# Splitting weight blocks with ScalarE and an adding transfer instead of VectorE, in a hybrid decoder layer

## The chip, the cores and the metric

The kernel runs on one core of a Trainium2 chip. The metric is the device time of one execution in microseconds (us); lower is better. The core has TensorE (matrix products, PE in the rows below; PEld is its weight load), VectorE (DVE), ScalarE (ACT), GpSimd (POOL) and SyncE (SP, which issues most transfers). Each engine takes its own instructions in order and waits for the others through semaphores.

## The reference

One decoder layer over 512 tokens of width 1024, in fp32. The normalised input goes through one projection (`w_in`), whose columns feed three groups of heads: NSA attention (a compressed branch, a selected branch and a window branch), RWKV-7 time mixing, and MoBA attention. Their outputs are joined by one output projection; a ConvGLU channel mixer and a final RMSNorm follow. Cut to what matters here:

```
h    = rmsnorm(x, attn_norm)
proj = h @ w_in                            # p_nsa, p_rw, p_moba
kc   = gelu(blocks(kc) @ cmp_w1[0]) @ cmp_w2[0]     # vc likewise with [1]
x    = x + concat(o_nsa, o_rw, o_moba) @ w_out
x    = x + conv_glu(rmsnorm(x, ffn_norm), ffn_w_in, ...)
out  = rmsnorm(x, final_norm)
```

With 512 tokens the selected branch takes every block and the window covers every earlier token, so the kernel computes both as causal attention.

## The kernel before, in words

Products are computed to about fp32 accuracy from a reduced-precision format (fp32r): every operand is split into a high part (the value rounded to fp32r) and a low part (the value minus its high part), and a product is three products, high by high, high by low and low by high (`mm3`, lines 240 to 242).

The weights of the layer's first half come in 70 blocks of 128 x 512 (256 KB): 38 of the input projection (19 projections of 128 columns, two blocks each), 16 of the hidden layer of the compression (8 blocks each for values, `hv`, and keys, `hk`) and 16 of the output projection. A block is loaded by SP into a tile `wraw` (six buffers). `wunit` casts it on ScalarE to the high tile `whi` (line 211, six buffers) and subtracts on VectorE to get the low tile `wlo` (line 212, five buffers). `wnext` hands the next block to whoever needs one and keeps a list of blocks already split, two long. The blocks come in the order of `ORDER`: ks, r1, v1, k1, q0, cv, ck (two each), hv (eight), q1, kw (two each), hk (eight), and then the rest; `nv` stands in between with loads and splits of its own (lines 732 and 733, tile `vw`). The first 30 blocks thus reach to the fourth block of hk.

The work of the first half is written as streams (Python generators): `w_stream` (the weight products), `rw_run` (two RWKV pairs), `cmp_attention`, `att_stream` (scores and softmax of nine pairs of heads, one after the other) and `val_stream` (their values). Each stream yields an estimate of the time until its next step (`CW`, `CATT` = 2.5 and so on), and `merge` takes the stream that is due first. The order so found is the program's order. The framework that lays out the engines' queues may still move an instruction ahead of earlier ones of its engine when its inputs are there first: the program's order is a priority, and the queues are made anew whenever an instruction changes. The same framework puts in every wait, those for a free buffer included.

Names that the text below uses: the first 16 loads (`xr`, `fraw`) and four projections run before the streams start. `s` is a score tile, `qt` the split query (line 702), written after the evacuation `P` (line 696). `Y`, `TA`, `GA`, `AR` and `Nc` belong to RWKV: `Y` (line 573) is a step of a triangular inverse; `Nc` (line 505) comes back from a round trip through memory and is used by `DvT` (line 508). `blk` holds the compression's blocks: POOL clears a column of each (line 890), VectorE fills it (line 896) and splits it (`bhl`, line 902). `ph` is the hidden layer's accumulator (lines 917 and 918). The RWKV gate products wait for a sigmoid on ScalarE (line 1062). POOL also computes reciprocal roots (lines 293, 392, 673, 862). From about 300 us on the ConvGLU mixer runs, whose splits are its own.

Of the kernel before, what the change touches and what calls it, by code (L numbers as in the profile page):

```python
# [24 lines left out]
CW, CRW0, CRW1, CATT, CVAL, CFIN, CCMP, CCA, RWLAG = 1.25, 3.45, 3.57, 2.5, 1.28, 4.05, 3.17, 1.69, 0  # L25
CT = 2.51
NR = 5
WARM = 5
KOUT, EARLY2, NEARLY2 = 1, 3, 2
LAG = 2  # L30
DMS = [0, 4, 1, 5, 2, 6, 3, 7]
# [4 lines left out]
F32 = mybir.dt.float32  # L36
F32R = mybir.dt.float32r
AF = mybir.ActivationFunctionType
OP = mybir.AluOpType
# [39 lines left out]
def cap(name):  # L79
    return CAPS.get(name, CDEF)  # L80
# [11 lines left out]
def hybrid_layer(ctx: ExitStack, tc: tile.TileContext, xT, cst, cols, lora, fgain, wA, wVn, cw1,  # L92
                 wO, wF, wG, out, dbg=None):
    nc = tc.nc
    act, dve, pool, pe, sp = nc.scalar, nc.vector, nc.gpsimd, nc.tensor, nc.sync
# [7 lines left out]
    def mark(label):  # L103
        MARKS.append((label, nc.cur_bb.bb.instructions[-1].name))
# [7 lines left out]
    def bank(name):  # L112
        live[0] += 1
        return ps.tile([128, 512], F32, name=name, bufs=pcap(name))
# [8 lines left out]
    def r2(name, shape=(128, 512), dt=F32):  # L123
        return sb.tile(list(shape), dt, name=name, bufs=cap(name))
# [69 lines left out]
    p0 = bank("rs")  # L194
    for i in range(WARM):
        pe.matmul(p0[:, 0:256], idle[:, 0:128], idle, start=True, stop=True)
# [8 lines left out]
    rcol = fixe(4)  # L205


    def wunit(raw, w):
        hi = sb.tile([128, 512], F32R, name="whi", bufs=cap("whi"))
        lo = sb.tile([128, 512], F32R, name="wlo", bufs=cap("wlo"))  # L210
        act.copy(hi[:, :w], raw)  # L211
        dve.tensor_tensor(lo[:, :w], raw, hi[:, :w].bitcast(F32), op=OP.subtract)  # L212
        return hi, lo

    def wload(src, w=512):
        raw = r2("wraw")
        sp.dma_start(raw[:, :w], src)
        return raw


    wsrc, wready = [], []
# [5 lines left out]

    def wsplit():
        src, m = wsrc.pop(0)
        wready.append(wunit(wload(src, m)[:, 0:m], m))  # L230

    def wnext():
        while len(wready) < 2 and wsrc:
            wsplit()
        return wready.pop(0)

# [23 lines left out]
    for z in SEQ:  # L260
# [13 lines left out]
        for k, i in new:  # L274
            n = sum(o[1] == i for o in order1)
# [31 lines left out]
    def proj_fm(box):  # L307
        yield from want()
        p = bank("mm")
        for u in range(2):  # L310
            hi, lo = wnext()
            for k in range(4 * u, 4 * u + 4):
                c = slice((k - 4 * u) * 128, (k - 4 * u + 1) * 128)
                mm3(p, (hi[:, c], lo[:, c]), (xh[k], xl[k]), k == 0, k == KT - 1)
                yield CW
        box.append(p)
# [457 lines left out]
    def soft(qt, kk, par, sums, mid):  # L774
        kh, kl, lo = kk
        two, three = r2("prob"), r2("prob")
        pt_ = two[:, 384:512], mid[:, par * 256:par * 256 + 256], two[:, 0:384], three
        Ps = []
        for i in range(NT):
            n = (i + 1) * 128  # L780
            yield from want()
            s_ = bank("s")
            qs = slice(i * 128, (i + 1) * 128)
            pe.matmul(s_[:, 0:n], qt[:, qs], kh[:, 0:n], start=True, stop=False)
            pe.matmul(s_[:, 0:n], qt[:, qs], kl[:, 0:n], start=False, stop=True)  # L785
            P = pt_[i]
            m = sm("m", 1)
            dve.tensor_tensor_reduce(out=P, in0=s_[:, 0:n], in1=con("cmask")[:, 512 - n:512], scale=1.0,  # L788
                                     scalar=3e38, op0=OP.add, op1=OP.min, accum_out=m)
            done()  # L790
            act.activation(P, P, AF.Exp, bias=m, scale=-1.0, accum_out=sums[:, i, par:par + 1])  # L791
            Ps.append(P)
            yield CATT
        return Ps
# [112 lines left out]
    def hidden(kv):  # L907
        while bhls[kv] is None:
            yield None
        bhl = bhls[kv]  # L910
        yield from want()
        ph = bank("ph")
        for u in range(8):
            hi, lo = wnext()
            for i in range(2):
                tp = u * 2 + i
                pe.matmul(ph[:, 0:256], bhl[tp // 4][:, tp % 4, :], hi[:, i * 256:(i + 1) * 256], start=tp == 0, stop=False)
                pe.matmul(ph[:, 0:256], bhl[tp // 4][:, tp % 4, :], lo[:, i * 256:(i + 1) * 256], start=False, stop=tp == 15)
            yield CW
        spawn(compressed(kv, ph))  # L920
# [198 lines left out]
    def w_out(part, dm, k0, k1):  # L1119
# [7 lines left out]
        for k in range(k0, k1):  # L1127
            while oT[k] is None:
                yield None
            if (k - k0) % 4 == 0:  # L1130
                hi, lo = wnext()
            c = slice((k - k0) % 4 * 128, ((k - k0) % 4 + 1) * 128)
            mm3(p, (hi[:, c], lo[:, c]), oT[k], k == k0, k == k1 - 1)
            yield CW
# [59 lines left out]
    def sums_tile():  # L1194
        return sm("sums", 8).rearrange("p (t h) -> p t h", h=2)
# [10 lines left out]
    def fin_nsa(j, b, OPt, sums, ob):  # L1206
        mark(f'fnsa{j}.{b}')
        c = sm("coef", 8)
        cv = c.rearrange("p (t h) -> p t h", h=2)
        dve.reciprocal(cv, sums)  # L1210
        o1 = 6 * j + b
        dve.tensor_tensor(cv, cv, gates[:, :, o1:o1 + 4:3], op=OP.mult)
        t = yield from scaled(OPt, c)
        ob.append(t)
        if len(ob) < 2:
            return
        while not cadone[0]:
            yield None
        yield CFIN
        at('ob').tensor_tensor(ob[0], ob[0], ob[1], op=OP.add)  # L1220
        yield from want()
        oc = bank("oc")
        for i in range(NT):
            pe.matmul(oc[:, i * 128:(i + 1) * 128], PT[j][:, i, :], Vbd[j], start=True, stop=True)
        yield CFIN
        dve.tensor_tensor(ob[0], ob[0], oc, op=OP.add)
        done()
        yield CFIN
        yield from finish_pair(ob[0], col("nsa_gain", j), j)

    def fin_moba(j, OPt, sums):
        mark(f'fmoba{j}')
        r = sm("coef", 8)
        dve.reciprocal(r, sums.rearrange("p t h -> p (t h)"))
        t = yield from scaled(OPt, r)
        yield CFIN
        yield from finish_pair(t, col("moba_gain", j), 5 + j)

    def att_stream():
        for kind, j, b in HEADS:  # L1240
            fold = ENG[f"F{kind}{j}{b}"] == 'p'
            OPt, sums = (r2("OPt"), r2("OPt") if fold else None, fold), sums_tile()
            if b < 2:
                ob = []
            while len(queue) > QMAX:
                yield None
            Ps, vs, mid = [], [], r2("prob")
            for par in range(2):
                h = 2 * j + par
                if kind == "n":  # L1250
                    kk = (ks, kw)[b - 1]
                    while qn[h] is None or not kk or not vn:
                        yield None
                    q_, k_, v_ = qn[h], kk[h // 3], vn[(b - 1) * 2 + h // 3]
                else:
                    while j not in mq or j not in mk or j not in mv:
                        yield None
                    q_, k_, v_ = mq[j][par], mk[j][par], mv[j][par]
                mark(f'soft{kind}{j}.{b}.{par}')
                vs.append(v_)  # L1260
                P = yield from soft(q_, k_, par, sums, mid)
                Ps.append(P)
            fin = fin_nsa(j, b, OPt, sums, ob) if kind == "n" else fin_moba(j, OPt, sums)
            queue.append((Ps, vs, OPt, fin, f'{kind}{j}.{b}'))
        queue.append(None)
# [14 lines left out]
    spawn(rw_run(0))  # L1280
    spawn(cmp_attention())
    spawn(att_stream())
    spawn(val_stream())
    merge()
# [267 lines left out]
```

## Time and profile before

| | us |
|---|---|
| median of 3 runs | 730.33 (729.77 to 731.89) |
| the profiled execution, its own time | 731.48 |
| its span in the profile | 729.4 |
| TensorE busy | 705.4 (97%) |
| VectorE busy | 627.0 (86%) |
| ScalarE busy | 415.3 (57%) |
| POOL busy | 30.8 (4%) |

The span is the profiled execution from its first to its last recorded instruction. A busy time counts an engine's instructions without overlap; the rest of the span is idle. The mean granted clock of TensorE was 0.986 of full speed. In the rows a name like `wlo<-wraw,whi` is output and inputs, `x30` a count, and what stands behind `<-` in brackets is what ended an idle time.

### The profile page before, as it was taken

What the parts mean: (1) busy time and instruction counts of PE and PEld (TensorE: products, weight loads), DVE (VectorE), ACT (ScalarE), POOL (GpSimd) and SP (SyncE); (2) the same over time, 40 slices, a digit from 0 to 9 for tenths busy, and PEclk for the clock granted to TensorE, in tenths of its full rate; (3) what the DMA queues carried; (4) which work ended last, traced back from release to release, by engine and by line L of the source; (5) the groups of instructions that cost most, each with busy time, mean ns of one, the idle gap of its engine ahead of it and who ended that gap; (6) DMA issues with size and microseconds to landing.
All of it is one profiled execution on the core that took longest, in us unless ns stands there. A gap on an engine that the chain in (4) does not pass through costs nothing. (4 is left out here: it accounts for less than half of the span.)

```text
span 729.4 us, 13565 instructions
## 1 busy us (share of the span) xinstructions
PE 705.4 (97%) x5156; PEld 613.6 (84%) x5156; DVE 627.0 (86%) x1377; ACT 415.3 (57%) x862; POOL 30.8 (4%) x46
## 2 busy tenths in 40 slices
PE   9999988899999999999999999999999999999995
PEld 6777867678788788888899899999999999998884
DVE  6579679878897999797999999999999999999804
ACT  8475434465656877774766546455564555657403
POOL 4010100000000000011000000000000000000001
PEclk9989989999999999999999999999999999999999
DMA  9622021513110022024246333323333333346003
GB/s 328 193 87 80 13 50 49 140 65 117 44 44 30 1 59 73 30 72 145 74 144 218 97 107 102 116 87 102 97 108 101 102 103 110 98 126 201 1 1 115
DMA packets 44800, 69.86 MB, mean 96 GB/s; under 512 B 10688, under 2 KB 12352, under 8 KB 44736
## 3 DMA queue, kind: packets, MB, share of 16 engines
q1 hardware_dynamic: 44016, 67.95, 29.4%
q10 hardware_dynamic: 720, 1.06, 0.4%
q8 instruction: 40, 0.66, 0.4%
q14 instruction: 24, 0.20, 0.1%
HBM read 64.40 MB, written 4.59 MB: 95 GB/s over the span
## 5 line engine op out<-in xcount | busy, mean ns | idle before, releaser
L1301 ACT CAST ah<-S 128x512 fp32r<-128x512 f32 x88 | 54.5, 621 | 57.6 <-DVE S L1296 57.6
L240 PE MATMUL mm<-xh,whi 128*128 128x512 f32 x152 | 69.6, 458 | 0.0
L241 PE MATMUL acc<-dn,dn 128*128 128x512 f32 (+1 forms) x173 | 64.3, 372 | 0.0
L242 PE MATMUL acc<-dn,dn 128*128 128x512 f32 (+1 forms) x173 | 63.8, 371 | 0.0
L242 PE MATMUL mm<-xh,wlo 128*128 128x512 f32 x152 | 61.8, 406 | 0.0
L241 PE MATMUL mm<-xl,whi 128*128 128x512 f32 x152 | 61.5, 404 | 0.0
L1302 DVE TENSOR_TENSOR al<-S,ah 128x512 fp32r<-128x512 f32 x88 | 58.7, 682 | 0.7 <-ACT ah L1301 0.6
L791 ACT ACTIVATE prob<-prob,fixed 128x128 f32<-128x128 f32 (+1 forms) x72 | 40.5, 563 | 28.5 <-DVE fixed L788 26.5
L240 PE MATMUL acc<-dn,dn 128*128 128x512 f32 (+1 forms) x173 | 54.9, 371 | 0.0
L211 ACT CAST whi<-wraw 128x512 fp32r<-128x512 f32 x70 | 42.6, 618 | 19.8 <-PE mm L241 14.1
L212 DVE TENSOR_TENSOR wlo<-wraw,whi 128x512 fp32r<-128x512 f32 x70 | 47.3, 682 | 3.6 <-PE mm L242 2.2
L240 PE MATMUL pB<-bh,ah 128*128 128x256 f32 x172 | 50.1, 291 | 0.1
L242 PE MATMUL pB<-bh,al 128*128 128x256 f32 x172 | 48.6, 283 | 1.1 <-DVE al L1302 1.0
L242 PE MATMUL pC<-bh,al 128*128 128x256 f32 x172 | 48.5, 282 | 0.3 <-DVE al L1302 0.3
L240 PE MATMUL pC<-bh,ah 128*128 128x256 f32 x172 | 48.5, 282 | 0.2 <-ACT ah L1301 0.2
L241 PE MATMUL pB<-bl,ah 128*128 128x256 f32 x172 | 48.3, 281 | 0.0
L241 PE MATMUL pC<-bl,ah 128*128 128x256 f32 x172 | 48.1, 280 | 0.0
L1302 DVE TENSOR_TENSOR al<-wraw,ah 128x512 fp32r<-128x512 f32 x66 | 43.4, 681 | 0.0
L823 ACT CAST ph<-pt 128x512 fp32r<-128x512 f32 (+3 forms) x72 | 29.7, 425 | 23.3 <-PE pt L816 22.4
L788 DVE CUSTOM_DVE_ANT_0 prob<-s,early 128x128 f32<-128x128 f32 (+1 forms) x72 | 34.7, 483 | 6.6 <-PE s L785 5.0
L1301 ACT CAST ah<-wraw 128x512 fp32r<-128x512 f32 x66 | 36.8, 618 | 1.4 <-DVE x L1135 1.3
L241 PEld LDWEIGHTS acc<-dn,dn 128*128 128x128 f32 x173 | 32.6, 188 | 5.3 <-DVE dn L1365 0.2
(400 smaller groups left out, 2211.8 us busy)
## 6 DMA issues: line engine op xcount, KB each, us to landing
wraw<-in_wF_dram SPq DMA_DIRECT2D x88, 256.0 KB, 2.7
wraw<-in_wG_dram SPq DMA_DIRECT2D x44, 256.0 KB, 3.0
wraw<-in_wA_dram SPq DMA_DIRECT2D x38, 256.0 KB, 3.0
xr<-in_xT_dram SPq DMA_DIRECT2D x16, 256.0 KB, 4.1
wraw<-in_cw_dram SPq DMA_DIRECT2D x16, 256.0 KB, 3.3
wraw<-in_wO_dram SPq DMA_DIRECT2D x16, 256.0 KB, 2.6
fraw<-in_wA_dram SPq DMA_DIRECT2D x8, 256.0 KB, 5.2
x2d<-x2o SPq DMA_DIRECT2D x8, 256.0 KB, 3.3
```

Of the source, the lines that this page charges most:

```text
L211: act.copy(hi[:, :w], raw)
L212: dve.tensor_tensor(lo[:, :w], raw, hi[:, :w].bitcast(F32), op=OP.subtract)
L240: pe.matmul(o, ah, bh, start=first, stop=False)
L241: pe.matmul(o, ah, bl, start=False, stop=False)
L242: pe.matmul(o, al, bh, start=False, stop=last)
L788: dve.tensor_tensor_reduce(out=P, in0=s_[:, 0:n], in1=con("cmask")[:, 512 - n:512], scale=1.0, scalar=3e38, op0=OP.add, op1=OP.min, accum_ ...
L791: act.activation(P, P, AF.Exp, bias=m, scale=-1.0, accum_out=sums[:, i, par:par + 1])
L823: act.copy(h, t_[:, 0:n])
L1301: act.copy(h, src)
L1302: at(f'L{i}').tensor_tensor(l, src, h.bitcast(F32), op=OP.subtract)
```

## The change

For the first 30 blocks VectorE's subtraction goes. ScalarE multiplies the block by -1 into `wlo` (which rounds it, so that `wlo` holds minus the high part), and POOL issues a transfer that adds the block, read from memory a second time, onto `wlo`. `wnext` keeps four blocks split instead of two; this holds for all 70 blocks. And `att_stream` yields two more steps of `CATT` before the scores of its first head.

```
+NADD, WAHEAD = 30, 4
...
-    def wunit(raw, w):
+    wcnt = [0]
+
+    def wunit(raw, w, src):
         hi = sb.tile([128, 512], F32R, name="whi", bufs=cap("whi"))
         lo = sb.tile([128, 512], F32R, name="wlo", bufs=cap("wlo"))
         act.copy(hi[:, :w], raw)
-        dve.tensor_tensor(lo[:, :w], raw, hi[:, :w].bitcast(F32), op=OP.subtract)
+        wcnt[0] += 1
+        if wcnt[0] <= NADD:
+
+            act.mul(lo[:, :w], raw, -1.0)
+            pool.dma_start(lo[:, :w], src.bitcast(F32R), accum_op=OP.add)
+        else:
+            dve.tensor_tensor(lo[:, :w], raw, hi[:, :w].bitcast(F32), op=OP.subtract)
         return hi, lo
...
-        wready.append(wunit(wload(src, m)[:, 0:m], m))
+        wready.append(wunit(wload(src, m)[:, 0:m], m, src))
 
     def wnext():
-        while len(wready) < 2 and wsrc:
+        while len(wready) < WAHEAD and wsrc:
...
                     q_, k_, v_ = mq[j][par], mk[j][par], mv[j][par]
+                if (kind, j, b, par) == ("n", 0, 1, 0):
+
+                    yield 2 * CATT
                 mark(f'soft{kind}{j}.{b}.{par}')
```

## Rows read from the trace of the kernel before

**Rows 1.** The page: busy time of TensorE and VectorE, share of the span.
```profile
span 729.4 us, 13565 instructions
PE 705.4 (97%) x5156; PEld 613.6 (84%) x5156; DVE 627.0 (86%) x1377; ACT 415.3 (57%) x862; POOL 30.8 (4%) x46
```

**Rows 2.** Stages: length, busy PE, PEld, DVE, ACT, POOL (instructions), clock, transfer share, GB/s.
```profile
20.00:170.00 150.00, 140.96 (x1278) 112.48 (x1277) 115.83 (x297) 78.09 (x161) 5.50 (x8) 0.94 0.30 84
20.00:50.00 30.00, 28.86 (x124) 21.99 (x123) 17.61 (x35) 19.38 (x34) 3.05 (x2) 0.89 0.46 138
90.00:110.00 20.00, 16.66 (x167) 12.48 (x166) 13.43 (x33) 7.37 (x15) 0.00 (x0) 0.83 0.24 51
110.00:140.00 30.00, 25.44 (x341) 20.78 (x340) 27.99 (x82) 12.96 (x30) 0.39 (x3) 0.94 0.30 82
170.00:300.00 130.00, 127.41 (x974) 104.63 (x972) 113.14 (x313) 87.95 (x228) 6.54 (x4) 1.00 0.16 49
```

**Rows 3.** TensorE's waits, 0 to 250 us: total, times, longest.
```profile
PE s L784 <- DVE qt L702: 3.9, 2, 3.3
PE ph L918 <- DVE wlo L212: 2.5, 2, 2.1
PE rw L533 <- DVE Y L573: 1.7, 1, 1.7
...
PE rw L366 <- ACT rwin L1062: 0.6, 1, 0.6
```

**Rows 4.** TensorE in order of time: start, duration, what, idle before.
```profile
131.47 0.39 PE L918 MATMUL ph<-wlo,bhl 128*128 128x256 f32 x1 [2.06 <-DVE wlo L212]
...
134.71 0.79 PE L240 MATMUL mm<-xh,whi 128*128 128x512 f32 x1
...
136.79 0.39 PE L240 MATMUL mm<-xh,whi 128*128 128x512 f32 x1
```

**Rows 5.** VectorE in order of time.
```profile
115.00 0.68 DVE L212 TENSOR_TENSOR wlo<-wraw,whi 128x512 fp32r<-128x512 f32 x1
...
118.77 0.68 DVE L573 TENSOR_TENSOR Y<-rw,Dv 128x512 f32<-128x512 f32 x1
```

**Rows 6.** All engines in order of time, around the first score product.
```profile
91.50 0.76 DVE L508 TENSOR_TENSOR DvT<-Nc,early 128x256 f32<-128x256 f32 x2 [4.78 <-DMA Nc<-s]
...
93.25 0.69 DVE L696 SCALAR_TENSOR_TENSOR P<-mm,early 128x512 f32<-128x512 f32 x1
...
95.91 0.47 PE L784 MATMUL s<-kk,qt 128*128 128x128 f32 x1 [3.34 <-DVE qt L702]
...
97.58 0.79 PE L240 MATMUL mm<-xh,whi 128*128 128x512 f32 x1
```

**Rows 7.** The two splitting lines: duration in ns (min/median/max), first and last start.
```profile
L211 ACT CAST whi<-wraw x70: 602/620/639, 17.7 to 354.0; 128x512 fp32r<-128x512 f32 x70
L212 DVE TENSOR_TENSOR wlo<-wraw,whi x70: 641/682/694, 19.8 to 365.5; 128x512 fp32r<-128x512 f32 x70
```

**Rows 8.** VectorE's instructions on `wlo` alone, one stage: busy (count), clock, transfers.
```profile
110.00:140.00 30.00, 7.44 (x11) 0.94 0.30 82
```

**Rows 9.** POOL in order of time.
```profile
30.34 1.02 POOL L293 TENSOR_TENSOR early<-fixed 128x4 f32<-128x4 f32 x1 [11.57 <-DVE fixed L292]
...
115.04 0.14 POOL L890 MEMSET blk<- 128x16 f32 x1 [32.38 <-DVE bhl L902]
```

**Rows 10.** Transfers by line: KB each, median us from issue to landing.
```profile
wraw<-in_wA_dram SPq DMA_DIRECT2D x38, 256.0 KB, 3.0
...
x2t<-x2d SPq DMA_DIRECT2D x8, 256.0 KB, 3.6
```

**Rows 11.** The hidden layers' low products: duration in ns, first and last start.
```profile
L918 PE MATMUL ph<-wlo,bhl x32: 278/281/386, 117.5 to 166.8; 128*128 128x256 f32 x32
```

**Rows 12.** TensorE in order of time: the second hidden layer's first low product.
```profile
155.02 0.28 PE L918 MATMUL ph<-wlo,bhl 128*128 128x256 f32 x1
```

**Rows 13.** ScalarE's waits for a free high tile, whole span: total, times, longest.
```profile
ACT whi L211 <- PE mm L241: 14.1, 7, 4.7
```

## The prediction

> **What bounds the kernel now.** I read the page first. TensorE is busy 705.4 us of a span of 729.4 and VectorE 627.0 [rows 1]. So TensorE's own work sets the time, and a change elsewhere can only give back what TensorE loses: time in which it stands idle, and time at half clock (the lower of its two levels, 1.2 GHz against 2.4). Next the table by stage, for the stage that the change touches, 20 to 170 us [rows 2]. TensorE is busy 140.96 of 150 there, so 9.0 us are idle. A granted clock that is 0.11 short over 30 us, 0.17 short over 20 us and 0.06 short over 30 us has cost 3.3, 3.4 and 1.8 us of work, 8.5 in sum. Those 17.5 us are all that this stage has to give. From 170 to 300 TensorE is idle 2.6 of 130 us at full clock: behind the stage there is little to win and something to lose.
>
> Third, who ends TensorE's waits in 0 to 250 us [rows 3]. Four rows carry nearly all: the first score product of attention waits for VectorE's `qt` (3.9 us, one wait of 3.3); the compression's hidden layer for `wlo`, the very subtraction that the change takes away (2.5, one of 2.1); RWKV for `Y`, VectorE too (1.7); and the LoRA gate for ScalarE's sigmoid (0.6).
>
> Last the order of time around these waits. At 131.47 us TensorE has stood 2.06 us for `wlo`, and at 134.71 a weight product takes 0.79 where the same line takes 0.39 at 136.79: the clock fell behind the gap [rows 4]. On VectorE the subtractions stand in line between RWKV's and the blocks' work, one at 115.00 ahead of the late `Y` at 118.77 [rows 5]. The gap of 3.34 us at 95.9 has another cause: VectorE stood 4.78 us for a transfer of RWKV's triangular block (`Nc`), with the query's evacuation queued behind it; the weight products that follow at 97.58 run at half speed [rows 6].
>
> **The change part by part.**
>
> *VectorE loses 30 subtractions.* One takes 0.68 us [rows 7], so 20.5 us go. Eleven of them start in the tightest stage, 110 to 140 us, where VectorE is busy 27.99 of 30 and gives up 7.44 [rows 2, 8]. What TensorE gets: the wait for `wlo`, 2.5, whole; of the 1.7 for `Y` what the subtractions ahead of it take, one or two of 0.68, say 0.9; and of the 1.8 of clock in that stage half, 0.9, since some small gaps stay. **Term 1: 4.3 us gained**; bounds 2.5 (the named wait alone) and 6.4 (all 4.6 idle and 1.8 clock).
>
> *Attention's first head begins two planner steps later.* The wait at 95.9 is that head's first product. Put behind other ready work it would cost nothing: the weight products at 97.58 waited only for their turn. At stake are the 3.3 idle and the 3.4 of clock in 90 to 110 us [rows 2, 6]. The engines' order is made anew, and neither the transfer that VectorE waited for nor its place in VectorE's order need change; between none and all I take half. **Term 2: 3.3 gained**, bounds 0 and 6.7.
>
> *ScalarE gains 30 multiplies.* The nearest row is its cast of the same tile, 0.62 us [rows 7]: 18.6 us onto the 78.1 that it is busy in 150 us [rows 2]. It stays at 64%, so its idle time hides them, except where TensorE waits for ScalarE already: the gate's sigmoid. One multiply queued ahead of it costs 0.6, three 1.9. **Term 3: 0.6 lost**, bounds 0 and 1.9.
>
> *POOL gains 30 adding transfers.* None is in the trace. POOL's part of one: the nearest row is its power of 128x4, 1.02 us [rows 9]; bounds nothing and twice that; I take 1.0. To land: a plain 256 KB load takes 3.0 us, and one that must also read its target at most two such transfers in turn, 3.0 and 3.6 [rows 10]; I take 4.0, nearer to the one transfer that it is. With the multiply a low tile takes 5.6 us to fill, against 1.3 now (cast and subtraction), bounds 3.6 and 9.3. The cover is the lookahead: four blocks ready, five `wlo` buffers. Filled in turn, five buffers give a block each 5.6 / 5 = 1.1 us (1.9 at the upper bound). TensorE asks fastest in the second hidden layer, 8 blocks from 155.0 to 166.8, 1.5 us each [rows 11, 12]; a projection's block, 12 products of 512 columns, lasts longer. At my value the cover holds. At the upper bound 12 hidden-layer blocks lose 0.4 each, 4.3 us in sum. Some one block will come late in a new order. **Term 4: 1.0 lost**, bounds 0 and 4.3. The transfers read 7.9 MB more; the DMA engines are busy 0.30 of this stage [rows 2], so that stays hidden.
>
> One rule of the Trainium skill speaks against this part ("SBUF — State Buffer", "SBUF: two separate sides"): POOL writes the descriptors of its own transfers, and is locked out of SBUF while VectorE runs a two-port operation such as an fp32 copy. No run here shows it yet. By it an add would wait out a copy, not the operations on two tensors that make up most of VectorE's time there, and the sum would stay; were the lock wider than the page says, VectorE's 93% in 110 to 140 us would make every add late there. I give the rival of late adds a little more for it.
>
> *Splits stand four blocks ahead, for all 70 blocks.* ScalarE already waits 14.1 us in seven waits for TensorE to free a `whi` buffer [rows 13]. Issued two blocks earlier against the same six and five buffers, such waits come more often, with exponentials and evacuations queued behind them. ScalarE (88 of 130 us in 170 to 300) has room; VectorE, at 113 of 130, has less. **Term 5: 1.0 lost**, bounds 0 and 3.0 (as much again as TensorE idles there now).
>
> Sum: 4.3 + 3.3 - 0.6 - 1.0 - 1.0 = 5.0 us. The profiled execution took 731.48, so 726.5; the median of the runs, 730.33, lies 1.15 below the profiled one, so **725.3**.
>
> **The rivals.**
>
> *Late adds (slower).* POOL takes its work in order, and between 82 us and the end of the first hidden layer stand three clears of `blk`, each waiting for VectorE: the first until 115.04, for 32.4 us [rows 9]. An add queued behind the first starts at 115.2 and lands at 120.2, where TensorE now reads the first hidden-layer `wlo` at 117.5 [rows 11]: 2.7 late. With the three clears, and each 2.7 to 5 late, 8 to 15 us; I take 10, and the 2.5 of term 1 is gone. That is 731.5 - 5.0 + 9.0 + 2.5 = 738.0, on the median's scale 736.9. It decides once the adds' lateness passes the gains, some 6 us. Against it: the adds' sources are ready long before, and nothing says that they stand behind the clears.
>
> *No change.* Either VectorE's relief is off the path beyond the 2.5 us named (2.5 - 0.6 - 1.0 - 1.0: 0.1 faster), or the later head pushes back attention's chain of nine heads, and the two steps of 2.5 us that term 2 borrowed are paid at its end (5.0 - 5.0). Both give 730.3. For it: VectorE's 87% in 170 to 300 us. Against: TensorE is full there, so a later head only changes what it does meanwhile.
>
> *All of it.* VectorE lighter by a fifth in the stage, all of term 1's and term 2's upper bounds come, 13.1 us: 717.2. For it: every large wait in rows 3 but the sigmoid's ends on VectorE. Against: RWKV's chain and its transfers stay.
>
> **How the numbers follow.** Forecast 0.48, all of it 0.12, no change 0.22, late adds 0.18. The forecast's own range is 722 to 728. The sum of the unfavourable bounds (2.5 + 0 - 1.9 - 4.3 - 3.0) is 6.7 slower, 737; that of the favourable ones 717.2. Cutting the outermost at both ends, the range is 717.5 to 736. A measurement of this kernel tells about 0.3%, 2.2 us, from no change: below 728.1 lie the forecast but for 0.04 and all of the third rival, 0.56; within 2.2 us lie that 0.04 and most of the no-change case, 0.20; the rest of that case and the late adds are slower, 0.24.
>
> **What would show it.** Term 1: no wait of TensorE on `wlo` in 110 to 140 us, VectorE there near 21 to 24 of 30, and a granted clock above 0.94. Term 2: the first score product without a gap of 3 us ahead of it, and a clock in 90 to 110 us near 1. Term 3: the wait for the sigmoid near 1.2. Term 4: adds that land within some 5 us and TensorE's waits on them under 1 us each. Term 5: 170 to 300 us with TensorE idle no more than 4 us. The prediction is wrong if an add takes over 9 us from multiply to landing, if POOL's clears hold the adds, or if new gaps of the reordered RWKV chain bring the clock down elsewhere.

## The result and the profile after

The changed kernel takes **734.79 us** (median of 6 runs, 732.22 to 735.62) against 730.5 for the kernel before on the same chip (6 runs, 729.77 to 731.89): a ratio of 1.0056 (95% interval 1.004 to 1.0073), some 4 us slower. The forecast was 725.3, faster; the time lies inside the forecast's range of 717.5 to 736, but on the slow side of the kernel before. The profiled execution has a span of 733.2 us, 3.8 more than before. In three kernels of the experiments (e1, e4 and e7 there) one execution took far longer than the rest (2219, 2359 and 842 us); the ratios leave these out, and the profiles of e1 and e7 are of one more execution each.

The page first, busy time and share of the span; it answers to [rows 1].

```profile
span 733.2 us, 13656 instructions
PE 706.7 (96%) x5156; PEld 613.6 (84%) x5156; DVE 610.4 (83%) x1347; ACT 431.3 (59%) x892; POOL 55.9 (8%) x76
```

VectorE has lost 16.6 us of work, ScalarE has gained 16.0 and POOL 25.1. TensorE does what it did. The stages, with the columns of [rows 2]:

```profile
20.00:170.00 150.00, 138.56 (x1272) 109.75 (x1271) 97.90 (x265) 92.32 (x190) 30.84 (x39) 0.95 0.62 139
20.00:50.00 30.00, 27.50 (x119) 21.05 (x118) 10.20 (x21) 18.20 (x33) 7.62 (x11) 0.93 0.77 187
90.00:110.00 20.00, 19.93 (x247) 15.00 (x246) 14.41 (x36) 9.51 (x20) 3.52 (x4) 1.00 0.62 106
110.00:140.00 30.00, 22.77 (x300) 18.67 (x298) 20.88 (x71) 18.43 (x39) 9.08 (x13) 0.89 0.86 183
170.00:300.00 130.00, 127.27 (x970) 104.38 (x970) 112.18 (x311) 86.66 (x224) 6.58 (x4) 1.00 0.15 48
```

In 90 to 110 us all has come that term 2 hoped for: TensorE stands 0.07 us in place of 3.34, at full clock. In 110 to 140 us VectorE is light, 20.88 in place of 27.99, and yet TensorE does less, 22.77 in place of 25.44, and the clock is 0.89 in place of 0.94. The column before the last is the news: the DMA engines are busy 0.62 of the stage in place of 0.30, 0.77 of the opening in place of 0.46, and 0.86 of 110 to 140 us in place of 0.30. What ended TensorE's waits, 0 to 400 us (total, times, longest):

```profile
PE ph L927 <- DMA wlo<-in_cw_dram: 5.7, 3, 3.5
PE rw L364 <- ACT rwin L1070: 1.7, 1, 1.7
PE rw L542 <- DVE Y L582: 1.5, 1, 1.5
...
PE rw L375 <- ACT rwin L1071: 0.8, 1, 0.8
```

The wait of the hidden layer for the subtraction [rows 3] is now one for the add, and more than twice as long. The transfers of the page: queue, packets, MB, share of 16 engines; then issues with KB each and median us to landing. The last fence holds two rows of the kernel before that are not shown above.

```profile
q1 hardware_dynamic: 44016, 67.95, 29.2%
q0 software_dynamic: 4320, 7.87, 6.5%
...
wlo<-in_wA_dram POOLq DMA_DIRECT2D x18, 256.0 KB, 7.3
wlo<-in_cw_dram POOLq DMA_DIRECT2D x12, 256.0 KB, 5.3
wraw<-in_wVn_dram SPq DMA_DIRECT2D x8, 137.0 KB, 6.4
...
early<-in_lora_dram SPq DMA_DIRECT2D x1, 128.0 KB, 11.5
```

```profile
wraw<-in_wVn_dram SPq DMA_DIRECT2D x8, 137.0 KB, 3.4
...
early<-in_lora_dram SPq DMA_DIRECT2D x1, 128.0 KB, 3.6
```

An add holds the sixteen engines for 6.5% of 733.2 us / 30 = 1.59 us; SP's loads hold them 0.83 us for the same 256 KB (29.2% of 733.2 us for 67.95 MB). And loads that have nothing to do with the adds land two and three times as late in the opening. The transfers' view of 10 to 40 us shows why: first the engines' busy share (in tenths) and the rate in 40 slices, then the queues in that window.

```profile
DMA  9999999999989899789999999999999999894016
GB/s 399 410 407 399 410 404 407 399 391 384 341 233 365 349 360 288 210 262 262 254 224 240 257 239 243 227 236 230 262 255 270 361 383 363 199 200 81 8 24 174
...
q1 hardware_dynamic: 4043, 6.96, 66.7%
q0 software_dynamic: 864, 1.57, 29.0%
```

The engines are full up to 35 us. The first add is issued at 18.95 us, and from 22 us on the rate is some 240 GB/s in place of 400, with the engines as busy as ahead of it (with plain transfers in place of the adds, e7 below, it is 270 to 390): they spend 29.0% of the window on adds that bring 1.57 of its 8.56 MB. Who waits for it stands in ScalarE's order of time, changed kernel and kernel before:

```profile
31.21 0.42 ACT L741 CAST vw<-wraw 128x274 fp32r<-128x274 f32 x1 [7.38 <-DMA wraw<-in_wVn_dram]
...
38.38 0.58 ACT L312 COPY early<-rb 128x512 f32<-128x512 f32 x1
...
43.92 0.63 ACT L1071 ACTIVATE rwin<-rwin 64x512 f32<-64x512 f32 x1
```

```profile
32.61 0.59 ACT L303 COPY early<-rb 128x512 f32<-128x512 f32 x1 [6.61 <-PE rb L300]
...
38.11 0.63 ACT L1062 ACTIVATE rwin<-rwin 64x512 f32<-64x512 f32 x1
```

ScalarE stands 7.38 us for a load of `nv`, its copy of `rb` starts 5.8 us later than before and the gate's sigmoid 5.8 later: RWKV's chain begins late. The second place is the hidden layer, in TensorE's order of time, where [rows 4] stood:

```profile
129.62 0.39 PE L927 MATMUL ph<-wlo,bhl 128*128 128x256 f32 x1 [3.54 <-DMA wlo<-in_cw_dram]
...
134.40 0.79 PE L249 MATMUL mm<-xh,whi 128*128 128x512 f32 x1
```

It is the picture of before with the names changed: a gap, and behind it a weight product at 0.79 us, half clock, where 0.39 is usual.

### The profile page after: what moved, and what is told of

Read it like the earlier page. It is cut to its first block, busy times and chain, and to the rows that moved or that the text cites. A ratio compares the mean times of both kernels' runs of the same rounds, so it can differ in the third digit from the quotient of the medians.

```text
span 733.2 us, 13656 instructions
## 1 busy us (share of the span) xinstructions
PE 706.7 (96%) x5156; PEld 613.6 (84%) x5156; DVE 610.4 (83%) x1347; ACT 431.3 (59%) x892; POOL 55.9 (8%) x76
## 3 DMA queue, kind: packets, MB, share of 16 engines
q1 hardware_dynamic: 44016, 67.95, 29.2%
## 4 chain that ended last, share of the span: by engine, by line
PE 73%; DVE 12%; DMA 6%; ACT 4%; issue 3%; POOL 1%; SPq 0%; POOLq 0%; ACTq 0%; DVEq 0%
PE mm L249 6%; PE mm L250 6%; PE mm L251 6%; PE acc L250 5%; PE acc L251 5%; PE acc L249 5%; PE pB L249 3%; PE ot L813 3%; PE pC L249 3%; PE pB L251 3%; PE pB L250 2%; PE pC L251 2%; PE pC L250 2%; PE pt L825 2%; PE pA L250 2%
## 5 line engine op out<-in xcount | busy, mean ns | idle before, releaser
L1363 ACT ACTIVATE cv<-ge,fixed 128x512 f32<-128x512 f32 x22 | 18.0, 818 | 32.4 <-DVE ge L1361 32.4
L250 PEld LDWEIGHTS acc<-dn,dn 128*128 128x128 f32 x173 | 32.5, 188 | 5.3 <-DVE dn L1377 0.2
L251 PEld LDWEIGHTS acc<-dn,dn 128*128 128x128 f32 x173 | 32.6, 188 | 5.2
```

The costliest lines, as they stand in the source:

```text
L250: pe.matmul(o, ah, bl, start=False, stop=False)
L251: pe.matmul(o, al, bh, start=False, stop=last)
L1363: act.activation(c, ge, AF.Identity, scale=col("conv_w", 44 + j), bias=col("conv_b", j))
```

## The experiments

Each ratio is against the kernel before on the same chip, with a 95% interval in brackets; a per cent is 7.3 us. "Faster" and "slower" in us go by the ratio, not by the medians. A difference between two kernels is that of their ratios, and behind its ± stands the root of the sum of the squares of their half intervals. All kernels are the changed one with the edit shown; e1 to e12 are their names.

**The parts alone.** The later head alone (e1):

```
-NADD, WAHEAD = 30, 4
+NADD, WAHEAD = 0, 2
```

> The kernel before with the later head alone (no adds, lookahead two). Theory A (the adds cost, the later head pays): the gap of 3.3 us ahead of the first score product and the half clock in 90 to 110 us go, the wait on wlo in the hidden layer (2.5 us) stays; 3 to 6 us faster than before, near 726. Theory B (the loss is the accident of a new order at the start of the channel mixer, whatever the edit): within 2 us of before, with a fall of the clock near 395 us. Rival C (the later head is paid back at the end of attention): no change, 730.

> The later head alone once more, for an undisturbed profile. Idle of TensorE in 90 to 110 us below 1 us and clock 1.00 there; from the first product of the output projection to the last stage 416 to 417 us if the fall of the clock at 395 us is absent, 419 if it is there.

Measured: 725.48 us, ratio 0.9928 [0.9908, 0.9948], 5.3 us faster; one more execution took 724.36. The gap is gone as in the changed kernel; its row of 90 to 110 us:

```profile
90.00:110.00 20.00, 19.48 (x247) 14.91 (x245) 19.46 (x50) 8.05 (x17) 0.13 (x1) 1.00 0.24 64
```

Of the kernels that leave nothing out this is the fastest, ahead of both the one before and the changed one: the two added lines in `att_stream`, without the rest.

The lookahead alone, without adds and without the later head (e2):

```
-NADD, WAHEAD = 30, 4
+NADD, WAHEAD = 0, 4
-                if (kind, j, b, par) == ("n", 0, 1, 0):
-                    yield 2 * CATT
```

> The kernel before with the lookahead of four alone. Theory A: the lookahead is not what costs; within 2 us of 730.5, and ScalarE's waits for a free high tile near the 14 us of before. Rival (the lookahead costs): 2 to 5 us slower, with more of ScalarE's and VectorE's time spent waiting for TensorE to free a tile.

Measured: 731.89 us, 1.0023 [1.0008, 1.0037], 1.7 slower.

The adds alone, lookahead of two, no later head (e3: `NADD, WAHEAD = 30, 2`, the same two lines removed):

> The kernel before with the 30 adds alone (lookahead two, no later head). Theory A: the adds are late with two blocks ahead even more than with four; TensorE waits for adds 8 us or more, 737 to 745. Theory B: the adds cost nothing of their own; 730 to 732.

Measured: 737.51 us, 1.0091 [1.0057, 1.0125], 6.6 slower. Lookahead and later head without adds (e4: `NADD, WAHEAD = 0, 4`):

> The changed kernel without the adds: lookahead four and later head, subtraction on VectorE. Theory A: it keeps the later head's gain and loses the adds' cost: 725 to 728. Theory B: 732 to 735 like the changed kernel, with the fall of the clock near 395 us.

Measured: 727.58 us, 0.9966 [0.9951, 0.9981], 2.5 faster. So the adds in place of the subtractions cost 0.90% (± 0.22), 6.6 us, with the other two parts (against e4) as without them (e3). With e3's 6.6 the parts add up: -2.5 + 6.6 = 4.1 slower.

**Where the adds cost.** By the blocks that have them. First the opening spared, blocks 1 to 8 by VectorE (e5):

```
-        if wcnt[0] <= NADD:
+        if 8 < wcnt[0] <= NADD:
```

> The changed kernel with VectorE's subtraction for blocks 1 to 8, adds for 9 to 30 only. Theory A1 (the opening: the first adds crowd the DMA engines while the first loads still run, and RWKV's chain starts late): loads of the opening land in 3 to 4 us again, the gate's sigmoid is no longer waited for 1.7 us, 730 to 732. Theory A2 (only the hidden layer's late adds cost): 734 as the changed kernel.

Measured: 728.23 us, 0.9978 [0.996, 0.9996], 1.6 faster than before and 0.78% (± 0.24), 5.7 us, better than the changed kernel. In its rows the load in the opening is back at its old place, while the hidden layer still waits for adds:

```profile
early<-in_lora_dram SPq DMA_DIRECT2D x1, 128.0 KB, 3.4
```

```profile
PE ph L927 <- DMA wlo<-in_cw_dram: 4.3, 3, 3.0
```

Then the hidden layer spared, adds for the 18 projection blocks alone (e6):

```
-        if wcnt[0] <= NADD:
+        if wcnt[0] <= NADD and not (15 <= wcnt[0] <= 22 or wcnt[0] >= 27):
```

> The changed kernel with VectorE's subtraction for the 12 hidden-layer blocks among the first 30, adds for the 18 projection blocks only. Theory A2: the waits of 5.7 us on adds go, 729 to 731. Theory A1 (the opening): 733 to 735, no better than the changed kernel.

Measured: 734.93 us, 1.0082 [1.006, 1.0104], no better than the changed kernel. The waits of 5.7 us are gone, and TensorE stands for others in their place, 2.6 us of it for the add of a projection's block; the opening stays as late as it was (its `rb` product starts at 35.0 us, before at 31.4). Then adds for the first eight blocks alone (e10: `NADD, WAHEAD = 8, 4`):

> The changed kernel with adds for blocks 1 to 8 alone, the opening's. Theory A1 (the opening is the larger part of the adds' cost): 3 to 6 us slower than the version without adds, 731 to 734, with the gate chain late by 3 us or more. Rival (the cost is spread over the 30): 728 to 729.5, a quarter of the 7 us.

Measured: 729.01 us (726.26 to 732.63, 12 runs), 0.9994 [0.9975, 1.0013]: below the 731 to 734 that I had expected. Against e4 the opening's eight adds cost 0.28% (± 0.24), 2.0 us; by e5 taking them away gives 5.7 back. The profiled execution of this kernel is the slowest of its twelve, so its span says little; its opening is that of the changed kernel (the 128 KB load lands after 12.0 us).

So the first eight adds alone cost 2.0 us, the other 22 alone 0.9 (e5 against e4, 0.12% ± 0.23), and all 30 together 6.6: the two places don't add up to a sum of fixed shares. Each of these kernels also has an order of its own.

**What it is about an add.** A plain transfer of the same block into the same tile, in the same place of the same queue (e7); `wlo` then holds the block itself, so the low parts of the 30 blocks are left out:

```
-            pool.dma_start(lo[:, :w], src.bitcast(F32R), accum_op=OP.add)
+            pool.dma_start(lo[:, :w], src.bitcast(F32R))
```

> The changed kernel with plain transfers from POOL where it adds (the low tile then holds the whole block, so the sums are others; every engine's order is the same). Theory A3 (an adding transfer holds the DMA engines twice as long as a plain one of the same bytes, and this makes it late): the software queue's share falls from 6.5% to some 3.3%, its transfers land within 4 us, the waits on them fall below 2 us, 729 to 732. Rival (POOL's own issue, 0.86 us, and the queue's place make it late): landing stays over 5 us and the time within 1 us of the changed kernel's 734.8.

> The plain transfers once more, for an undisturbed profile. The engines' order is that of the changed kernel. If the fall of the clock at 395 us belongs to this order, it is here too (granted clock 0.93 in 385 to 410); if it belongs to how late the stage arrives, it may be gone.

Measured: 726.68 us, 0.9964 [0.9949, 0.9979]; one more execution took 727.31. All five engines carry out the same instructions in the same order as in the changed kernel, and the time is 0.92% (± 0.22), 6.7 us, less. Its transfers and waits:

```profile
q0 software_dynamic: 4320, 7.87, 3.9%
...
wlo<-in_wA_dram POOLq DMA_DIRECT2D x18, 256.0 KB, 4.5
wlo<-in_cw_dram POOLq DMA_DIRECT2D x12, 256.0 KB, 4.0
...
early<-in_lora_dram SPq DMA_DIRECT2D x1, 128.0 KB, 9.4
```

```profile
PE ph L927 <- DMA wlo<-in_cw_dram: 2.6, 2, 1.4
```

3.9% of its 725.5 us by 30 is 0.94 us of all engines for one, against 1.59 with the addition; it lands earlier, and so does the load beside it.

ScalarE's multiply kept, VectorE adding the block onto it, no transfer (e8):

```
-            pool.dma_start(lo[:, :w], src.bitcast(F32R), accum_op=OP.add)
+            dve.tensor_tensor(lo[:, :w], raw, lo[:, :w].bitcast(F32), op=OP.add)
```

> The changed kernel with ScalarE's multiplies kept, and VectorE adding the block onto the low tile in place of the transfer. Theory A (the transfers cost): within 1.5 us of the version without adds, 726 to 729. Rival (ScalarE's 18.6 us of multiplies cost, waits in its queue): 730 to 734.

Measured: 727.53 us, 0.9979 [0.9962, 0.9996]. Against e4 that is 0.13%, 1 us, for the 30 multiplies, with intervals that overlap. The multiply alone, with no transfer and no subtraction (e9; the low part is left out, and `wlo` holds minus the high part):

> The changed kernel without the transfers: the low tile of the first 30 blocks holds the multiplied block and nothing is added (the sums are others). It is what VectorE's relief would be worth if the adds were free. Term 1 as predicted (4.3 us): 4 us below the version without adds, 722 to 724. Rival (the relief is off the path: RWKV's chain and its transfers keep TensorE's pace): 725 to 728, within 1.5 us of the version without adds and of the plain transfers.

Measured: 722.98 us, 0.9919 [0.9895, 0.9942]. This is what the change would give if the adds were free: 0.47% (± 0.28), 3.4 us, better than e4 and 1.37% (± 0.29), 10.0 us, better than the changed kernel. Its hidden layer has no wait for `wlo`, and VectorE is as light as term 1 described. But TensorE does no more in 110 to 140 us than before (25.44), since other waits stand there, the longer one for ScalarE's `TA`:

```profile
110.00:140.00 30.00, 25.35 (x344) 20.39 (x344) 20.29 (x65) 21.53 (x49) 0.25 (x2) 0.94 0.38 106
...
PE rw L541 <- ACT TA L551: 3.1, 1, 3.1
PE rw L541 <- DVE Y L581: 1.6, 1, 1.6
```

**Load or lateness.** An add may cost because TensorE waits until it lands, or because it keeps the engines from the loads. The changed kernel and e7 run one order, so each product of TensorE can be set beside its twin. Three of them, in the changed kernel and then in e7:

```profile
42.66 0.69 PE L364 MATMUL rw<-rwin,early 32*128 32x512 f32 x1 [1.69 <-ACT rwin L1070]
...
77.32 0.39 PE L249 MATMUL mm<-vw,xh 128*128 128x274 f32 x1 [1.34 <-DVE fixed L398]
...
131.54 0.58 PE L927 MATMUL ph<-wlo,bhl 128*128 128x256 f32 x1 [1.19 <-DMA wlo<-in_cw_dram]
```

```profile
41.09 0.69 PE L364 MATMUL rw<-rwin,early 32*128 32x512 f32 x1
...
73.68 0.40 PE L249 MATMUL mm<-vw,xh 128*128 128x274 f32 x1
...
124.40 0.39 PE L927 MATMUL ph<-wlo,bhl 128*128 128x256 f32 x1 [1.41 <-DMA wlo<-in_cw_dram]
```

Up to 41 us TensorE is 0.2 us ahead of e7. It is 1.6 behind at the gate's product and 2.2 at 50 us; 3.6 at 78 us, after VectorE has stood 2.9 us in place of 1.4 for a round trip of RWKV's (`NB`); 4.0 at 110; 8.4 at 140, after the hidden layer's late adds and the half clock behind them; and 7.7 at the end. So in this pair about half of what the addition costs arises ahead of the hidden layer, from transfers of others that land late, and about half in it, from adds that land late.

In the last two kernels nobody reads what POOL's transfer brought: TensorE takes the high tile a second time for the first 30 blocks, whose low parts are so left out (e11).

```
-        return hi, lo
+        return hi, (hi if wcnt[0] <= NADD else lo)
```

> The changed kernel with all its 30 multiplies and 30 adding transfers, but TensorE reads the high tile in place of the low one for these blocks, so no engine reads what an add brought (the low parts of 30 blocks are left out of the products). What stays is the adds' load on the transfer engines and a buffer's wait for its last add. Theory A, the adds cost by keeping the transfer engines from the loads: at least half of the 10.0 us between the changed kernel and the one without transfers stays, ratio 0.997 to 1.004, and the loads in 20 to 50 us land late as before (the 128 KB lora load near 11 us). Theory B, the adds cost by landing after TensorE asks for them: as without transfers, ratio 0.990 to 0.994.

The second with the plain transfer of e7 besides (e12):

> As e11, with a plain transfer of POOL in place of each adding one, read by nobody either. Theory A: the transfer holds the engines 0.94 us in place of 1.59, so it lies 1 to 4 us below e11, ratio 0.992 to 0.998. Theory B: the same as e11 within 1 us, ratio 0.990 to 0.994.

Measured: 744.41 us, 1.0196 [1.0172, 1.022] (e11), and 731.99 us, 1.0035 [1.0016, 1.0053] (e12). e11 is far slower than either theory had it, and e12 slower than both too; neither has a wait of TensorE for an add. What I had not foreseen: with nobody to wait for, the framework splits blocks earlier, and 13 transfers of POOL are issued in 10 to 50 us in place of 8. POOL's order of time in e11, idle before in brackets:

```profile
24.03 0.86 POOL L219 DMA_DIRECT2D wlo<-in_wA_dram  x1 [0.18 <-issue]
25.07 2.64 POOL L219 DMA_DIRECT2D wlo<-in_wA_dram  x3 [0.18 <-issue]
28.47 0.86 POOL L219 DMA_DIRECT2D wlo<-in_wA_dram  x1 [0.75 <-DMA wlo<-in_wA_dram]
```

And the stage 20 to 50 us, the transfers of the whole span, and TensorE's longest waits of e11:

```profile
20.00:50.00 30.00, 22.98 (x107) 18.80 (x106) 5.96 (x15) 14.19 (x31) 11.52 (x15) 0.91 1.04 253
```

```profile
wraw<-in_wVn_dram SPq DMA_DIRECT2D x8, 137.0 KB, 12.2
...
early<-in_lora_dram SPq DMA_DIRECT2D x1, 128.0 KB, 13.3
```

```profile
PE mm L249 <- DVE ex L343: 7.0, 1, 7.0
PE mm L249 <- ACT a L370: 5.5, 1, 5.5
PE rw L542 <- ACT TA L552: 4.4, 1, 4.4
```

TensorE loses 7.0 of the 30 us of the opening, for RWKV's inputs, none of it for an add. The two kernels' engines run the same order, so the 1.6% (± 0.3), 12 us, between them is what the addition costs where TensorE waits for no add. Most of it is in place by 50 us, where e11's TensorE is 6.7 us behind e12's. That is the load on the transfer engines and, not told apart from it, POOL's longer issue and the time that POOL and ScalarE wait until a buffer's last transfer has landed (10.8 us in e11, 5.8 in e12). Theory B's forecast, both at 0.990 to 0.994, was wrong: transfers that nobody waits for cost a lot. But the order here crowds the opening with more of them than the changed kernel's does, so the sizes don't carry over to it.

## Why the prediction was wrong

**Term 4, the adds, is the step that failed.** It put them at 1.0 us, at most 4.3. They cost 10.0 us against no transfer (e9), and of that the addition, against a plain transfer, makes 6.7 (e7). From the kernel before over e1, e4 and e9 to the changed one the steps are 5.3 gained by the later head, 2.8 lost by the lookahead beside it, 3.4 gained by the relief with its multiplies and 10.0 lost by the adds, 4.1 lost in all: term 4 alone turns the sign. Two sentences of the step were wrong.

- "the DMA engines are busy 0.30 of this stage [rows 2], so that stays hidden." That was a mean over 150 us. The same rows show 0.46 for the opening [rows 2], and the rate of 10 to 40 us shows full engines up to 35 us. The first adds meet the loads of `nv` and LoRA there, and RWKV's chain, on which much of the later order hangs, starts 5.8 us late. By bytes the adds move 7.9 MB; by engine time they count as 15 MB, since 256 KB hold the engines 1.59 us in place of 0.83.
- The landing, 4.0 us by two rows whose medians run over the whole span [rows 10]: measured 7.3 and 5.3 in the median, 9.1 in 10 to 40 us. With that a sign came that the prediction had named, an add that takes over 9 us from multiply to landing. The fill of five buffers that I had worked out with 5.6 us per tile did then fail, in the first hidden layer where I had looked at the second: 5.7 us of waits against the 4.3 of my upper bound.

The Trainium skill has a line that bears on each ("DMA: Bandwidth & Descriptors"). "SWDGE vs HWDGE vs iDMA" says that GpSimd's and SP's transfers feed different internal queues of the same sixteen engines, which take turns between them; the trace agrees that they share the engines, with SP's 128 KB load landing after 11.5 us in place of 3.6. "Rules for kernel authors" says that an adding transfer reads its target and writes it later; the 1.59 us against 0.94 fit that, though no run shows which step of it takes the time.

**Term 1, VectorE's relief,** 4.3 us: VectorE came to 20.88 us in 110 to 140 us, below the 21 to 24 predicted, and where the adds are out of the way (e9) the wait for `wlo` is gone. The rest of the mechanism did not show: `Y` keeps TensorE waiting 1.6 us as before, a wait of 3.1 for `TA` has come, and the clock of that stage is 0.94 as before. e9's 3.4 us against e4, with the multiplies' cost in it, is near the 3.7 of terms 1 and 3; but of the 5.5 us between their two profiled executions 2.9 come behind the first half (see term 5), where no subtraction was saved, so that the size fits is in part luck. In the changed kernel none of it reaches TensorE, whose wait passed from VectorE's `wlo` to the transfer's.

**Term 2, the later head,** 3.3 us: right in its mechanism and too small, 5.3 alone (e1), within its bounds. I took half since the transfer that VectorE waited for might not move; it did not have to (in e1 VectorE still stands 4.2 us for it), as TensorE had other work meanwhile.

**Term 3, the multiplies,** 0.6 us: about 1 (e8), not told from nothing. The wait for the gate's sigmoid (line 1071 now) came to 0.8 us where I expected 1.2; beside it stands one of 1.7 for the activation before it (line 1070), which runs late with the rest of that chain.

**Term 5, the lookahead,** 1.0 us: 1.7 alone (e2), within its bounds; 2.8 beside the later head (e4 against e1). TensorE idles 2.7 us in 170 to 300 us, as predicted. Some of its price falls later: from the last transposition of the first half (`xt`, near 380 us) to the first product on `dnt` (near 705 us) it is 323.5 us before, 323.4 in e1 and 322.9 in e9, but 325.7 in the changed kernel, 325.8 in e4 and 325.5 in e7. So 2.2 of the 3.8 us that the changed kernel's profiled execution is longer than the one before lie behind the first half. The seam at 385 to 410 us has waits and, in the changed kernel and e4, a dip of the clock; e7 has the changed kernel's order and no dip, so the dip is not the order's alone. e2, with the same lookahead, has 324.6 and e5 and e8, with the later head besides, 323.4 and 323.1, so the lost time goes with the order that came out and not with the adds. What in the order does it stays open.

**The rivals.** "Late adds" had the sign and, at 736.9, nearly the time, by luck: its mechanism was another. It had POOL's clears of `blk` hold the adds. All engines' waits name that once, for 3.7 us, and even that add's own multiply ended only at 121.96 us, 0.3 ahead of the issue at 122.25. The adds are issued right behind their multiplies, for which POOL waits:

```profile
POOL wlo L219 <- ACT wlo L218: 68.3, 21, 11.1
...
POOL wlo L219 <- DVE bhl L911: 3.7, 1, 3.7
```

They are late after their issue, in the engines. The lock-out that the prediction weighed from the Trainium skill ("SBUF — State Buffer", "SBUF: two separate sides") didn't show either: in 110 to 140 us, with VectorE busy 20.88 of 30, POOL's issues took 0.86 us as elsewhere; no run here isolates it. "All of it", at 717.2, was not reached with the transfers taken out, 722.98 (e9). "No change" has neither a mechanism here nor the time.

## What to carry to other kernels

Before work goes to the DMA engines, read their busy share and rate in the stretch where the first of the transfers fall, not in the mean of the stage, and price a transfer by the engine time that it holds, not by its bytes: one that adds counted here as nearly two of SP's. Ask then what other loads land late and which chain starts with them; a wait that is named for the new transfer, as in the hidden layer, can be half of the price or less. And time the parts of a mixed change singly: here two lines that only put off one head were worth 5.3 us, and the larger part took it away.

## What was not expected of the hardware

- A transfer of 128 x 512 fp32 from memory held the sixteen engines 0.83 us when SP issued it (by the mean over all of SP's bytes), 0.94 when POOL did, and 1.59 when POOL had it add to its target.
- POOL needed 0.86 us to issue an adding transfer of 128 x 512 (row at 24.03 us above) and 0.53 for a plain one (the median of 30 in e12).
- With the opening's seven adds under way the full engines moved some 240 GB/s in place of some 400; with plain transfers in their place 270 to 390 (e7).
